# Layer A of a hybrid decoder step: the score products of the even units moved directly behind the chain's visits, those of the odd units gathered in two visits instead of five

## The chip, the cores and the metric

The kernel runs on one core of one Trainium2 chip. The metric is the device time of one execution in microseconds (us), lower is better. All arithmetic is fp32; the large weight products are done as three products of split numbers (a high part and a low part of the weight, and of the activation).

## What is computed

One inference step of a two-layer decoder trunk, for a prompt group (16 meta rows and 256 prompt rows, L = 272) and a sample group (8 rows), N = 280 columns together, model width 2048, branch width 4096. Layer A is RWKV-7 time mixing, layer B is sliding-window attention. The change is in layer A, whose reference is a scan over the rows with one 64 by 64 state per head:

```python
def rwkv7_step(S, inp):
    r, d, k, v, kk, b = inp
    sa = jnp.einsum('bhij,bhj->bhi', S, kk)
    S = S * d[:, :, None, :] - sa[..., None] * b[:, :, None, :] + v[..., None] * k[:, :, None, :]
    return S, jnp.einsum('bhij,bhj->bhi', S, r)
```

Before the scan stand the projections r, k, v, z (`jnp.einsum('btpd,pde->btpe', xm[:, :, :4], w_rkvz)`, four matrices of 2048 by 4096) and two small low-rank products for the decay and for a; behind it a group norm per head, a gate with silu(z) and the output projection of 4096 by 2048.

## The kernel before, in words

**The scan in chunks.** The kernel does not step through 272 rows. It cuts them into five chunks (four of 64 rows, one of 16) and solves each chunk with matrix products. A unit is 4 heads (two tiles of 128 partitions, two heads in each); there are 16 units, and two units, an even and an odd one, make a pair. For each unit:

- `prep` (line 803) loads k, r, v and the key norms from DRAM, does the low-rank products (`ps_l`), the decays and the small tiles for the sample group (`sm`, `ps_sm`) and the bonus (`ps_bo`). `prep_e` (line 901) builds the factors `KB` and `E`.
- `scores` (line 927) forms the products of `KB` with `E`. Two blocks of 8 matmuls each (line 959, tile `ps_sc`) take two chunks each; a third block of 4 (line 976) takes the short chunk; then two groups of 10 transposes (line 996, `ps_bk`) turn `KB`. What leaves PSUM after a block: three copies on ScalarE for each half (lines 964 to 966, into `ND` and `N12`) and two masked products on VectorE (lines 967 and 969, back into `E` and into `RB`). The transposes leave by ScalarE copies into `BK` (line 998).

For each pair:

- `substitute` (line 1000) inverts 16 by 16 triangles on GpSimd and VectorE and lays the result into the diagonal of the tile `TT` with four ScalarE activations (line 1032).
- `solve` (line 1036) extends that to 64 by 64 in four visits of many small matmuls (`ps_so`, lines 1049, 1055, 1067, 1076), each with copies out between them.
- `chain` (line 1104) walks through the five chunks. A chunk has three visits: `ps_wu` and `ps_sy` from the state (lines 1133 and 1137), `ps_wu` with `TT` (line 1148) after a ScalarE copy `W`, and `ps_sy` (lines 1151 and 1153) after the copies `X`; then VectorE updates the state `FS`.
- `group_norm` (line 1195) finishes the rows of the pair and writes them to DRAM.

**The stream that carries the time.** All this is small work beside the large weight products, which `products` yields (line 650): for every weight tile a ScalarE cast makes the high part `whi` (line 177), VectorE makes the low part `wlo` (line 178), and TensorE does three matmuls of 128 by 128 against 280 columns (lines 199 to 201). `products` yields after every 6 of these matmuls; this is called a step here.

**Who decides the order.** `drive` (line 567) goes from step to step. At each step it asks every stream (epilogues, the main stream, preps, decodes, late gates and side streams) whether its turn has come, lets it record its instructions, and then lets `products` record the next 6 matmuls. A stream says with `yield n, need` that it wants its next turn n steps later and only when `need` holds. The order of TensorE is written out by this: it runs its instructions as they were recorded. The order on VectorE, ScalarE, GpSimd and the DMA queue of SyncE is chosen by a scheduler from what was recorded, with priorities (the main stream stands 2000 ahead). So a stream's instructions on TensorE come as a block between two steps; this block is called a visit here.

The main stream (`main`, line 610) runs a pair's `chain`, then the odd `scores` of the next pair, then its `solve`. The even `scores` of the next pair run as a side stream (`even_scores`, line 637), beside the chain, at steps of their own:

```python
        gap = iter((8, 3, 4, 3, 3) if odd else (8, 6, 6, 5, 4))
        turn = iter((0, odd, 0, odd, 0))
```

`gap` is the number of steps ahead of each of the five visits; `turn` picks the PSUM banks: the two banks of pool `pe`, or (in the second and fourth visit of an odd unit) one bank each of pools `pc` and `py`, which the chain uses otherwise.

Of the kernel before, what the change touches and what calls it, by code (L numbers as in the profile page):

```python
# [10 lines left out]
F32 = mybir.dt.float32  # L11
# [9 lines left out]
E = 4096  # L21
# [82 lines left out]
class Kernel:  # L104
# [462 lines left out]
    def drive(self, products, streams, begun, ahead=2000):  # L567
        self.samples = False
        live = [[g, *begun.get(g, (0, None))] for g in streams]

        now = streams[:2]
        more = True
        with self.pe_order():
            while more or self.later or len(live) > 1:
                for s in list(live):
# [15 lines left out]
                self.pos += 1  # L591

# [210 lines left out]
    def prep(self, u):  # L803
# [5 lines left out]
        p0 = 2 * u  # L809
# [3 lines left out]
        wa, ws = [], []  # L813
# [27 lines left out]
        self.spread(kk, self.kr[u // 4][4 * u % 16:4 * u % 16 + 4])  # L841
        for j in range(2):
# [29 lines left out]
        vT = w("vT", 4)  # L872
        dma(vT, self.vd[b][:, sl])
# [4 lines left out]
        yield 8, self.pp_free  # L878
# [48 lines left out]
    def scores(self, u):  # L927
# [3 lines left out]
        gap = iter((8, 3, 4, 3, 3) if odd else (8, 6, 6, 5, 4))  # L931
        turn = iter((0, odd, 0, odd, 0))
        banks = lambda nm: [self.bank(p, f"ps_{nm[0]}{q}{nm[1]}") for q, p in
                            enumerate((self.pc, self.py) if next(turn) else (self.pe, self.pe))]
# [14 lines left out]
        for c0 in (0, 2):  # L949
            cs = slice(c0, c0 + 2)  # L950
            yield next(gap)
            ps = [b.rearrange("p (a c t) -> p a c t", a=2, c=2) for b in banks(("sc", f"{c0}_{u}"))]

            with self.pe_order():
                for j in range(2):
                    for c in range(2):
                        for q in (1, 0):
                            o = 128 * (c0 + c)
                            nc.tensor.matmul(ps[q][:, j, c], KB[H(q), j, c0 + c, 64 * q:64 * q + 128],
                                             E[q][H(q), j, o:o + 128], start=True, stop=True)  # L960
# [10 lines left out]
        yield next(gap)  # L971
        ps = [b[:, :64].rearrange("p (a h t) -> p a h t", a=2, h=2) for b in banks(("sc", f"4_{u}"))]
        with self.pe_order():
# [4 lines left out]
        for q in range(2):  # L978
            pv, kr, br = ps[q], H(1 - q), H(q)
            r1 = slice(64 * q, 64 * q + 32)  # L980
            m = self.cst(C_MASK, 128, kr).rearrange("p (h t) -> p h t", h=2)[:, :, 0:16]
            A.copy(self.ND[r1, 16 + i0 // 4:18 + i0 // 4, 0:16], pv[r1, :, 0])
            tt(E[q][kr, :, 512:544].rearrange("p a (h t) -> p a h t", h=2), pv[kr],
               m.unsqueeze(1).to_broadcast((64, 2, 2, 16)), op=MU)
            tt(RB[br, :, 256:272], pv[br, :, 1],
               self.cst(C_MASK + 64, 16, br).unsqueeze(1).to_broadcast((64, 2, 16)), op=MU)
        if odd:
            self.substitute(u // 2)

        for j in range(2):  # L990
            yield next(gap)
            ps = [b[:, :320].rearrange("p (c t) -> p c t", c=5) for b in banks(("bk", f"{j}_{u}"))]
            with self.pe_order():
                for c in range(5):
                    for q in (1, 0):
# [857 lines left out]
```

## Time and profile before

| | us |
|---|---|
| median of 3 runs | 2206.55 |
| lowest and highest run | 2203.35 and 2210.55 |
| the profiled execution's own time | 2211.88 |
| its span from first to last instruction | 2209.9 |
| TensorE busy (share of the span) | 2122.6 (96%) |
| VectorE busy | 1711.5 (77%) |
| ScalarE busy | 1283.1 (58%) |
| GpSimd busy | 76.1 (3%) |

The granted TensorE clock is 0.988 of full speed over the span. The span has three parts: a first stage up to about 170 us, layer A's mixed stage (weight products with prep, scores, solve and chain between) up to about 1360 us, and then the output projection of layer A and all of layer B. The fp32 matmuls of the small work appear as two records each in the profile, so 8 matmuls are 16 records; transposes and the large products appear as one. In a row of the timeline, the first number is the start, the second the time from the start to the end of the merged records, and the shape behind the operation's name is first the part of the array that the weights fill (rows * columns) and then the moving operand. Ends on TensorE are modelled, starts are not: the time that a visit takes is read from the starts of the rows around it.

### The profile page before, as it was taken

The numbers are of one execution on the slowest core, as the hardware profiler recorded it, in microseconds if no ns is written. First come the engines' busy times: TensorE is split into PE (matmuls) and PEld (weight loads), VectorE is DVE, ScalarE is ACT, GpSimd is POOL, SyncE is SP. The second block draws the span as 40 slices with busy tenths as digits, with TensorE's granted clock in tenths as the row PEclk, the third lists the DMA queues.
The fourth block names the chain that finished last, engine by engine and source line by source line (L and its number), as shares of the span: only waits on it lengthen the run. The fifth ranks groups of instructions, "written<-read, shape, count | busy, mean of one in ns | idle before, by whom it ended". The sixth has DMA issues, their size and how long they took to land. (4 is left out here: it accounts for less than half of the span.)

```text
span 2209.9 us, 56367 instructions
## 1 busy us (share of the span) xinstructions
PE 2122.6 (96%) x21596; PEld 2013.0 (91%) x21596; DVE 1711.5 (77%) x4138; ACT 1283.1 (58%) x2961; POOL 76.1 (3%) x102
## 2 busy tenths in 40 slices
PE   6999999899999999989999999999999999999997
PEld 4898889899999898989998999999999999999997
DVE  5875756687778786789878787887888888888885
ACT  3556765577576665667766444564565556555443
POOL 0010000000000000000100000110000000000000
PEclk9999999999999999999999999999999999999999
DMA  7988576658675668766655858777554554577774
GB/s 238 342 262 252 174 224 208 197 173 259 198 227 177 186 211 260 228 211 185 200 176 155 275 181 272 239 215 208 154 162 144 154 157 129 164 213 241 230 226 136
DMA packets 424886, 455.40 MB, mean 206 GB/s; under 512 B 64280, under 2 KB 383320, under 8 KB 424224
## 3 DMA queue, kind: packets, MB, share of 16 engines
q1 hardware_dynamic: 423800, 449.51, 65.6%
q8 instruction: 169, 2.77, 0.5%
q10 hardware_dynamic: 816, 2.29, 0.3%
q14 instruction: 101, 0.83, 0.1%
HBM read 385.08 MB, written 70.73 MB: 206 GB/s over the span
## 5 line engine op out<-in xcount | busy, mean ns | idle before, releaser
L199 PE MATMUL ps_z<-mhlm,whi_z 128*128 128x280 f32 x512 | 159.5, 311 | 0.0
L199 PE MATMUL ps_q<-bmh,whi_qb 128*128 128x264 f32 x512 | 150.6, 294 | 1.8 <-ACT whi_qb L177 1.8
L201 PE MATMUL ps_z<-mhlm,wlo_z 128*128 128x280 f32 x512 | 150.6, 294 | 0.8 <-DVE wlo_z L178 0.8
L200 PE MATMUL ps_z<-mhlm,whi_z 128*128 128x280 f32 x512 | 150.5, 294 | 0.0
L201 PE MATMUL ps_q<-bmh,wlo_qb 128*128 128x264 f32 x512 | 146.5, 286 | 1.1 <-DVE wlo_qb L178 1.1
L199 PE MATMUL ps_z<-bmh,whi_zb 128*128 128x264 f32 x512 | 147.5, 288 | 0.0
L200 PE MATMUL ps_q<-bml,whi_qb 128*128 128x264 f32 x512 | 146.1, 285 | 0.0
L200 PE MATMUL ps_z<-bml,whi_zb 128*128 128x264 f32 x512 | 145.4, 284 | 0.0
L201 PE MATMUL ps_z<-bmh,wlo_zb 128*128 128x264 f32 x512 | 145.4, 284 | 0.0
L199 PE MATMUL ps_ob<-ghi,whi_ob 128*128 128x264 f32 x512 | 145.2, 284 | 0.0
L201 PE MATMUL ps_ob<-ghi,wlo_ob 128*128 128x264 f32 x512 | 144.8, 285 | 0.0
L200 PE MATMUL ps_ob<-glo,whi_ob 128*128 128x264 f32 x512 | 144.5, 283 | 0.0
L177 ACT CAST whi_ob<-raw_ob 128x512 fp32r<-128x512 f32 x128 | 79.2, 621 | 97.0 <-PE ps_ob L200 78.7
L178 DVE TENSOR_TENSOR wlo_r<-raw_r,whi_r 128x512 fp32r<-128x512 f32 x128 | 87.1, 687 | 60.8 <-ACT whi_r L177 59.2
L177 ACT CAST whi_oa<-raw_oa 128x512 fp32r<-128x512 f32 x128 | 78.3, 621 | 89.5 <-DMA raw_oa<-a_w_out 35.4
L178 DVE TENSOR_TENSOR wlo_v<-raw_v,whi_v 128x512 fp32r<-128x512 f32 x128 | 87.0, 687 | 52.7 <-ACT whi_v L177 51.1
L199 PE MATMUL ps_v<-mhlm,whi_v 128*128 128x280 f32 x384 | 122.5, 319 | 0.7 <-ACT whi_v L177 0.7
L199 PE MATMUL ps_k<-mhlm,whi_k 128*128 128x280 f32 x384 | 120.6, 314 | 0.0
L178 DVE TENSOR_TENSOR wlo_k<-raw_k,whi_k 128x512 fp32r<-128x512 f32 x112 | 76.2, 688 | 53.8 <-ACT whi_k L177 51.8
L178 DVE TENSOR_TENSOR wlo_z<-raw_z,whi_z 128x512 fp32r<-128x512 f32 x128 | 86.8, 685 | 36.5 <-ACT whi_z L177 36.3
L177 ACT CAST whi_zb<-raw_zb 128x512 fp32r<-128x512 f32 x128 | 78.3, 619 | 62.5 <-PE ps_z L200 41.9
L201 PE MATMUL ps_v<-mhlm,wlo_v 128*128 128x280 f32 x384 | 113.2, 295 | 0.2 <-DVE wlo_v L178 0.2
(479 smaller groups left out, 7725.2 us busy)
## 6 DMA issues: line engine op xcount, KB each, us to landing
raw_k<-a_w_rkvz SPq DMA_DIRECT2D x128, 256.0 KB
raw_v<-a_w_rkvz SPq DMA_DIRECT2D x128, 256.0 KB
raw_r<-a_w_rkvz SPq DMA_DIRECT2D x128, 256.0 KB
raw_z<-a_w_rkvz SPq DMA_DIRECT2D x128, 256.0 KB
raw_oa<-a_w_out SPq DMA_DIRECT2D x128, 256.0 KB
raw_qb<-b_w_qz SPq DMA_DIRECT2D x128, 256.0 KB
raw_zb<-b_w_qz SPq DMA_DIRECT2D x128, 256.0 KB
raw_ob<-b_w_o SPq DMA_DIRECT2D x128, 256.0 KB
```

Source lines behind the costliest of these rows:

```text
L177: self.nc.scalar.copy(hi, src)
L178: return self.nc.vector.tensor_tensor(lo, src, hi.bitcast(F32), op=ALU.subtract)
L199: mm(ps, wh, xh, start=start, stop=False)
L200: mm(ps, wh, xl, start=False, stop=False)
L201: return mm(ps, wl, xh, start=False, stop=stop)
```

## The change

Only the functions `drive`, `prep`, `scores`, `substitute`, `solve` and `chain` are touched. No instruction is added on any of the compute engines and none is removed; instructions are put in other places.

- **Even units.** The five visits become four, and each waits for `ride`: it is taken only at a step at which the chain has just recorded a visit (`vis == pos`), or when no chain is running. `drive` now asks the streams in a sorted order so that a riding stream comes last in its step. The gaps are 8, 6, 6, 5. The third visit holds the short block and the first group of transposes, which share the two banks (transposes in columns 0 to 319, the block in columns 320 to 383). All visits use the banks of `pe`.
- **Odd units.** Two visits: 8 steps after the chain both large blocks (the first into `pe`, the second into `pc` and `py`), 6 steps later the short block and both groups of transposes (`block`, `last` and `turned` record the matmuls, `block_out`, `last_out` and `turned_out` the same copies as before). `substitute` is recorded there, and `solve` begins 30 steps later (33 for the last two pairs) instead of 24 (27).
- **TT.** Its four diagonal activations move from `substitute` into `solve`, behind the first visit of `solve` and its copy `ET`.
- **Copies later.** In `prep` both low-rank weight loads are issued 3 steps ahead of their casts, the first work with the loaded `kk` comes 3 steps after its load, and the load of `vT` stands 3 steps ahead of the copies that read it, ahead of the decays for the units 0 to 3. The step counts behind are cut by the same amounts (7 to 4, 8 to 5).

```diff
@@ drive
+        self.vis, self.chain_on = -1, False
-                for s in list(live):
+                for s in sorted(live, key=lambda s: 0 if s[0] in now else 1 if s[2] == self.ride else 2):
...
+    def ride(self):
+        return self.vis == self.pos or not self.chain_on
@@ prep
             dma(raw, I[wn][0, :, p0 * 128:p0 * 128 + 256])
+            raws.append(raw)
+        if u:
+            yield 3
+        for i, raw in enumerate(raws):
...
-                yield 3 if i or j else 7 if u else 14, self.pp_free
+                yield 3 if i or j else 4 if u else 14, self.pp_free
...
         self.spread(kk, self.kr[u // 4][4 * u % 16:4 * u % 16 + 4])
+        if u < 4:
+            vT = w("vT", 4)
+            dma(vT, self.vd[b][:, sl])
+        yield 3
...
         if u >= 4:
             yield 0, self.after(0, ('g', u // 2 - 2))
-        vT = w("vT", 4)
-        dma(vT, self.vd[b][:, sl])
+            vT = w("vT", 4)
+            dma(vT, self.vd[b][:, sl])
+            yield 3
...
-        yield 8, self.pp_free
+        yield 5, self.pp_free
@@ scores
+        wide = lambda nm: [self.bank(p, f"ps_{nm}{q}_{u}") for q, p in enumerate((self.pc, self.py))]
+        near = lambda nm: [self.bank(self.pe, f"ps_{nm}{q}_{u}") for q in range(2)]
...
+        if odd:
+            yield 8
+            with self.pe_order():
+                p0 = block(0, near("sca"))
+                p2 = block(2, wide("scb"))
+            block_out(*p0)
+            block_out(*p2)
+            yield 6
+            with self.pe_order():
+                banks = near("sc4")
+                p4 = last([b[:, 320:384] for b in banks])
+                t0 = turned(0, banks)
+                t1 = turned(1, wide("bkb"))
+            last_out(p4)
+            self.substitute(u // 2)
+            turned_out(*t0)
+            turned_out(*t1)
+            return
+        for c0 in (0, 2):
+            yield 8 - c0, self.ride
+            with self.pe_order():
+                p = block(c0, near(f"sc{c0}"))
+            block_out(*p)
+        yield 6, self.ride
+        with self.pe_order():
+            banks = near("sc4")
+            p4 = last([b[:, 320:384] for b in banks])
+            t = turned(0, banks)
+        last_out(p4)
+        turned_out(*t)
+        yield 5, self.ride
+        with self.pe_order():
+            t = turned(1, near("bkb"))
+        turned_out(*t)
@@ substitute
-        TT = rp.tile([128, 20, 64], F32, tag="TT", name=f"TT{o}")
-        for b in range(4):
-            A.activation(TT[:, :, 16 * b:16 * b + 16], TR[:, :, 0:20].rearrange("p t i -> p i t"), AF.Copy,
-                         scale=self.cst(C_M64 + 16 * b, 1))
@@ solve
-        yield 24 if o < 5 else 27
+        yield 30 if o < 5 else 33
...
         V.tensor_copy(ET, ps[:, 0:256].rearrange("p (i s) -> p i s", s=16))
+        TT = self.TT = rp.tile([128, 20, 64], F32, tag="TT", name=f"TT{o}")
+        for b in range(4):
+            A.activation(TT[:, :, 16 * b:16 * b + 16], TR[:, :, 0:20].rearrange("p t i -> p i t"), AF.Copy,
+                         scale=self.cst(C_M64 + 16 * b, 1))
         yield 4
@@ chain, at its three visits
+            self.vis, self.chain_on = self.pos, True
+            self.vis = self.pos
+            self.vis, self.chain_on = self.pos, c < 4
```

More of the change, by code (lines that the diff above doesn't have):

```diff
@@ L930, in scores @@
         odd = u % 2
[L931 to L934, printed above, removed]
         V, A, G = nc.vector, nc.scalar, nc.gpsimd
@@ L970, in scores, with last @@
                    bc(self.cst(C_MASK + 64, 64, br), 64, 2, 2, 64), op=MU)
-        yield next(gap)
-        ps = [b[:, :64].rearrange("p (a h t) -> p a h t", a=2, h=2) for b in banks(("sc", f"4_{u}"))]
-        with self.pe_order():
+        def last(outs):
+            ps = [b.rearrange("p (a h t) -> p a h t", a=2, h=2) for b in outs]
             for j in range(2):
@@ L977, in scores @@
                                      start=True, stop=True)
[L978 to L995, printed above, removed]
-                        nc.tensor.transpose(ps[q][:, c], KB[H(q), j, c, 64 * q:64 * q + 128], self.ident[H(q), H(q)])
+            return ps
+        def last_out(ps):
+            for q in range(2):
+                pv, kr, br = ps[q], H(1 - q), H(q)
+                r1 = slice(64 * q, 64 * q + 32)
+                m = self.cst(C_MASK, 128, kr).rearrange("p (h t) -> p h t", h=2)[:, :, 0:16]
+                A.copy(self.ND[r1, 16 + i0 // 4:18 + i0 // 4, 0:16], pv[r1, :, 0])
+                tt(E[q][kr, :, 512:544].rearrange("p a (h t) -> p a h t", h=2), pv[kr],
+                   m.unsqueeze(1).to_broadcast((64, 2, 2, 16)), op=MU)
+                tt(RB[br, :, 256:272], pv[br, :, 1],
+                   self.cst(C_MASK + 64, 16, br).unsqueeze(1).to_broadcast((64, 2, 16)), op=MU)
@@ L1029, in substitute @@
         V.transpose(TR.rearrange("p t i -> p (t i)"), NL)
[L1030 to L1034 removed]
+        self.TN, self.TR = TN, TR
     def solve(self, o):
```

32 lines of the change are left out of this document (19 added, 13 removed).

## The prediction

> **What bounds the kernel now.** I read the page's busy times first, then the busy times of the middle stage alone, then TensorE's waits, and last the timeline of single visits on TensorE, because the page says nothing on what a visit costs.
>
> ```profile
> PE 2122.6 (96%) x21596; PEld 2013.0 (91%) x21596; DVE 1711.5 (77%) x4138; ACT 1283.1 (58%) x2961; POOL 76.1 (3%) x102
> ```
>
> ```profile
> 170.00:1360.00 1190.00, 1143.02 (x13855) 1072.61 (x13854) 900.24 (x2022) 757.20 (x1799) 37.64 (x47) 0.98 0.68 210
> ```
>
> TensorE is the bound, and in layer A's mixed stage (the second row: its length, then busy TensorE, weight loads, VectorE, ScalarE, GpSimd) it is idle for only 1190.0 - 1143.0 = 47 us. The change touches nothing outside this stage. So it can gain in two ways: fewer or cheaper visits, or less of these 47 us. They are scattered over many short waits, of which these are the ones that the change comes near:
>
> ```profile
> PE ps_so L1049 <- DVE TN L1028: 4.8, 3, 3.3
> PE ps_vt L797 <- ACT vk L799: 3.9, 2, 2.5
> PE ps_o L199 <- ACT whi_oa L177: 2.8, 1, 2.8
> PE ps_so L1055 <- DVE ET L1051: 2.5, 2, 2.1
> PE ps_bk L996 <- DVE RB L985: 1.6, 2, 1.2
> ```
>
> What a visit costs beside its matmuls is in the timeline of TensorE. The first rows are a chain's third visit that by chance has a score block behind it; then come a chain's first visit, a score block alone, a chain's second visit with transposes behind it by chance, and transposes alone:
>
> ```profile
> 317.95 0.29 PE L201 MATMUL ps_k<-mhlm,wlo_k 128*128 128x280 f32 x1
> 318.18 0.69 PE L1151 MATMUL ps_sy<-X,BK 128*64 128x64 f32 x16
> 318.79 0.68 PE L1153 MATMUL ps_sy<-X,RB 64*64 64x64 f32 x16
> 319.40 1.16 PE L959 MATMUL ps_sc<-E,KB 64*128 64x128 f32 x16
> 320.49 0.40 PE L199 MATMUL ps_k<-mhlm,whi_k 128*128 128x280 f32 x1
> ...
> 324.55 0.69 PE L1133 MATMUL ps_wu<-X,E 128*64 128x64 f32 x16
> 325.07 0.64 PE L1137 MATMUL ps_sy<-X,E 128*64 128x64 f32 x16
> ...
> 326.00 0.29 PE L201 MATMUL ps_k<-mhlm,wlo_k 128*128 128x280 f32 x1
> ...
> 326.38 0.29 PE L201 MATMUL ps_k<-mhlm,wlo_k 128*128 128x280 f32 x1
> 326.60 1.16 PE L959 MATMUL ps_sc<-E,KB 64*128 64x128 f32 x16
> 327.69 0.40 PE L199 MATMUL ps_k<-mhlm,whi_k 128*128 128x280 f32 x1
> 327.93 0.29 PE L200 MATMUL ps_k<-mhlm,whi_k 128*128 128x280 f32 x1
> ...
> 341.60 0.68 PE L1148 MATMUL ps_wu<-W,TT 64*64 64x64 f32 x16
> 342.21 0.53 PE L996 MATMUL ps_bk<-consts,KB 64*128 64x64 f32 x10
> ```
>
> Between visits three large matmuls take 326.38 - 326.00 = 0.38, so 0.13 each, and a step of six is 0.77. Around the lone block: the last large matmul starts 0.22 ahead of it instead of 0.13 (entry: 0.09), the block runs 327.69 - 326.60 = 1.09, and the second large matmul behind it starts 0.24 after the first instead of 0.13 (exit: 0.11). Behind the chain's visit the same block again takes 320.49 - 319.40 = 1.09, with no entry and no exit of its own. So a joined visit saves 0.09 + 0.11 = **0.20 us**, though the tile of the array changes (64\*64 to 64\*128). Where the tile does not change, it saves more: 16 records followed by others of the same tile take 325.07 - 324.55 = 0.52, followed by another tile 342.21 - 341.60 = 0.61, and 318.79 - 318.18 is 0.61 too. A change of tile thus costs 0.09, and a join without one saves 0.20 + 0.09 = **0.29 us**.
>
> The Trainium skill, TensorEngine Tiling (Array Packing), section Tiling Modes, says that a change of the tiling mode drains TensorE, while a change of the tile within a mode does not. By it the joins between unlike tiles would be worth little; the rows agree that a change costs something, with 0.09, but it is less than an exit and an entry.
>
> **The change part by part.**
>
> *Joined visits.* I counted joins in the instruction order of the two built programs; both have the same matmuls. Before, 6 score or transpose groups stand by chance directly behind a chain's group. After, 28 do, all with a change of tile: 18 score groups behind `ps_sy` and 3 behind `ps_wu`, 7 transpose groups behind `ps_sy`. That is 22 more at 0.20: 4.4 us. Groups of one tile (64\*128) that now touch: the two large blocks of the 8 odd units, the short block with the first transposes in all 16 units, the first with the second transposes in the 8 odd units: 32 at 0.29: 9.3 us. Sum: **13.7 us less on TensorE**, all of it on the path, since TensorE is the path. Bounds: for unlike joins behind `ps_wu` and `ps_sy` of 128\*64 no row exists; from nothing to 0.20 each. For like joins no score or transpose row exists either; between 0.20, the unlike price, and 0.36. The upper end: if the 16 records of a block started as densely as those of `ps_wu` inside a visit, the 1.09 of the block would fall by no more than 0.16 (its 1.16 less the last record's own time, over 15 gaps, times 16, is near 0.93). So 6 to 16 us; I take 13.7, nearest to the rows.
>
> *Odd units, bursts.* Both blocks leave PSUM together, and the second visit needs `pe` empty for the short block and `pc` and `py` for the second transposes.
>
> ```profile
> L967 DVE TENSOR_TENSOR E<-ps_sc,consts 64x512 f32<-64x512 f32 x64 | 43.8, 684 | 18.9 <-ACT N L966 14.1 <-PE ps_r L200 2.6 <-PE ps_z L201 1.2
> L969 DVE TENSOR_TENSOR RB<-ps_sc,consts 64x256 f32<-64x256 f32 x64 | 27.0, 422 | 0.9
> L178 DVE TENSOR_TENSOR wlo_v<-raw_v,whi_v 128x512 fp32r<-128x512 f32 x128 | 87.0, 687 | 52.7 <-ACT whi_v L177 51.1 <-PE ps_v L201 1.1
> ```
>
> VectorE needs 4 x 0.684 + 4 x 0.422 = 4.4 us for both blocks, and one or two low parts of 0.69 fall between: 5.1 to 5.8. The time from the end of the first visit to the first write into `pc` is 6 steps, 4.6, and about 0.9 for the short block and the first transposes: 5.5. That just fits when VectorE is free. It is not always:
>
> ```profile
> 382.38 1.16 PE L959 MATMUL ps_sc<-E,KB 64*128 64x128 f32 x16
> ```
>
> ```profile
> 383.59 1.76 DVE L1205 TENSOR_TENSOR Y<-Y,gvar 128x1536 f32<-128x1536 f32 x1
> 388.99 0.42 DVE L969 TENSOR_TENSOR RB<-ps_sc,consts 64x256 f32<-64x256 f32 x1
> ```
>
> Here the group norm's 1.76 us stood ahead, and the first block was out only 389.41 - 382.38 = 7.0 after it began. With the second block's 2.2 and one low part, 0.7, it is 9.9; the visit would want it at 2.2 + 5.5 = 7.7. Wait: 2.2. I estimate that two or three of eight units are like this: 5 us lost; bounds 0 and 8 x 2.2 = 17.6. Given back: the 1.6 of `ps_bk` on `RB` of the short block, since the next use of those banks is now `solve`, 30 steps later.
>
> *Even units, rides.* 28 visits of the chain get a block behind them. Queued behind it on ScalarE stand the chain's copies `X`:
>
> ```profile
> L965 ACT COPY ND<-ps_sc 32x128 f32<-32x128 f32 x64 | 16.5, 258 | 0.8
> L1150 ACT COPY X<-ps_wu 64x256 f32<-64x256 f32 x64 | 23.3, 365 | 18.2 <-PE ps_wu L1148 17.1
> L177 ACT CAST whi_v<-raw_v 128x512 fp32r<-128x512 f32 x128 | 78.5, 618 | 55.0 <-DMA raw_v<-a_w_rkvz 27.1 <-PE ps_v L200 19.5 <-PE ps_v L201 3.1
> ```
>
> In the built order six copies, 6 x 0.258 = 1.55, and a cast, 0.62, stand between `W` and the two `X`. They take 2.2 from the block's end; the chain's second visit begins two steps, 1.5, after it and needs some 0.8, so they are done when `X` may start. `X` takes 0.73, the third visit comes three steps, 2.3, later: 1.6 us of slack. Cost: nothing. Without that cover it is one for one, times 28.
>
> *TT.* Four activations move past the first visit of `solve`:
>
> ```profile
> L1032 ACT ACTIVATE TT<-TR,consts 128x320 f32<-128x320 f32 x32 | 25.4, 870 | 5.8 <-DVE TR L1029 5.8
> ```
>
> That is 3.5 us of ScalarE between the first and second visit, four steps or 3.1, and the first user is the copies behind the second. Those have seven steps, 5.4, to the third. So nothing is late. What goes is the 5.8 us in which ScalarE stood waiting for `TR` with casts and other copies queued behind. I credit 1.8 us of TensorE's waits behind it, an estimate; bounds 0 and the 7.3 of both `ps_so` rows above.
>
> *Loads.* SyncE's queue issues the same loads in nearly the same order; `vT` now stands three steps ahead of the copies from it. ScalarE's idle time for it, 15.9 us in 6 waits, is one source of late casts.
>
> ```profile
>   DMA vT<-vd: 15.9, 6
> ```
>
> But in the built order the copy from `vT` stands as many casts behind its load as before (counting weight loads on SyncE and casts on ScalarE), as the scheduler moved both. Cost and gain: nothing; bounds a gain of 3.9 (`ps_vt` above) and a loss of as much. The 3 steps ahead of the low-rank casts are taken out behind them. The chains end 8 steps earlier against the weight products, so the late gates and their loads meet other casts: 0, at most 2.8 either way (the `ps_o` row).
>
> **Sum.** -13.7 + 5.0 - 1.6 - 1.8 = -12.1. The profiled execution took 2211.88 (span 2209.9), 5.3 above the median of the three runs; I subtract from both: 2199.8 for a like execution, and **2194.5 us** against the median of 2206.55.
>
> **Rivals.**
>
> *Unlike joins save nothing.* If the drain at a change of tile from 128\*64 to 64\*128 costs a whole entry and exit, the 4.4 go: 2199. Against it speaks the block at 319.40. This is what the skill's rule, read strictly, gives. Chance 0.10.
>
> *All odd units wait.* If VectorE is late in all eight, 17.6 instead of 5.0: 2207, no change. For it: the fit of 5.1 to 5.8 into 5.5 is tight. Against: most low parts stand ahead of the burst in the built order, as casts run some four weight tiles ahead. Chance 0.14.
>
> *Slower: the rides hold the chain up.* The place is ScalarE between a block's copies and `X`, the price is one for one in 28 visits, and it decides once ScalarE is more than 1.6 late there. At 2.6 late each, 28 us are lost: 2222. Against: ScalarE is 757 of 1190 us busy. Chance 0.11.
>
> *More than forecast.* If the steps between loads and copies also take away the waits for `vT` and more of those for `TN` and `ET`, some 7 more: 2187. Chance 0.13.
>
> **How the numbers follow.** Forecast with 2189 to 2200 as its own range: 0.52. A change under 0.3% (6.6 us) is about what a measurement of this kernel cannot tell from none, so faster means below 2199.9. Faster: 0.52, 0.13, most of the unlike joins and a little of the third case: 0.73. Same: the rest of both: 0.16. Slower: 0.11. The range from 2184 to 2207 leaves out the rides and the outermost part of the better case.
>
> **What would show it.** The timeline of TensorE should show joined groups with starts 0.61 apart where the tile changes; a large block followed by another some 0.95 later, not 1.09; the short block and the transposes with no large matmul between. The second visit of odd units should show at most three waits for `E` or `RB`. `ps_bk`'s wait on `RB` of the short block, and ScalarE's wait for `TR` ahead of `TT`, should be gone. Idle time of TensorE in the mixed stage should stay between 43 and 53 us. The prediction is wrong if that idle time grows by over 8, with waits of `ps_sy` for `X` or of the transposes for `RB`, or if like joins save no more than 0.20.

## The result, and the profile after

The changed kernel takes 2243.65 us (median of four runs, 2238.49 to 2247.48) against 2208.55 for the kernel before on the same chip: a ratio of 1.0162, with a 95% interval of 1.0144 to 1.0180. It is slower by 35 us; 2194.5 had been predicted, with a range up to 2207. Its profiled execution took 2238.49 (span 2236.5, mean granted clock 0.978), that of the kernel before 2211.88 (span 2209.9, clock 0.988).

The page's line of busy times of the changed kernel tells nothing of it:

```profile
PE 2122.4 (95%) x21596; PEld 2022.3 (90%) x21596; DVE 1708.8 (76%) x4138; ACT 1285.1 (57%) x2961; POOL 72.2 (3%) x102
```

TensorE's busy time is what it was (2122.6). The loss shows in the mixed stage alone, in the table of busy times by stretch (changed kernel; length, then TensorE, weight loads, VectorE, ScalarE, GpSimd, granted clock, DMA share):

```profile
170.00:1360.00 1190.00, 1120.07 (x13712) 1058.99 (x13712) 884.89 (x1998) 750.28 (x1784) 33.34 (x47) 0.97 0.67 204
```

Two numbers of this row are worse than before: TensorE stands idle for 1190.0 - 1120.1 = 69.9 us instead of 47.0, and the granted clock is 0.97 instead of 0.98. TensorE's waits in this stage (changed kernel; who waits, for what, us in total, times, longest):

```profile
PE ps_so L1095 <- DVE TN L1078: 15.0, 3, 7.0
PE ps_so L1105 <- issue: 8.0, 4, 3.0
PE ps_wu L1184 <- ACT X L1220: 5.8, 5, 3.0
...
PE ps_so L1095 <- issue: 3.3, 1, 3.3
```

The first two visits of `solve` wait 15.0 + 8.0 + 3.3 = 26.3 us. In the kernel before, the same two waited 4.8 for `TN`, 2.5 for `ET` and, with no releaser named, 2.2 + 0.9, in all 10.4:

```profile
PE ps_so L1055 <- issue: 2.2, 3, 0.9
...
PE ps_so L1049 <- issue: 0.9, 1, 0.9
```

The waits with no releaser ("issue") are of another kind than those for `TN`: they are holes inside a visit. In the second visit at 427.20 of the changed kernel, 124 of the 128 records run, and then TensorE stands, though `ET` had been there since 425.99:

```profile
430.34 0.23 PE L1105 MATMUL ps_so<-TR,ET 32*16 32x16 f32 x4 [1.93 <-issue]
```

The other such waits of the two visits also fall between records of one visit; what they wait for, the profile does not show. No score or transpose visit of the changed kernel waits for `E` or `RB`.

The joins are there, as forecast. TensorE's timeline of the changed kernel: an odd unit's two large blocks, then, at another place, an even unit's block riding behind a chain's first visit:

```profile
931.48 0.29 PE L201 MATMUL ps_z<-mhlm,wlo_z 128*128 128x280 f32 x1
931.69 1.16 PE L968 MATMUL ps_sca<-E,KB 64*128 64x128 f32 x16
932.69 1.06 PE L968 MATMUL ps_scb<-E,KB 64*128 64x128 f32 x16
933.68 0.39 PE L199 MATMUL ps_z<-mhlm,whi_z 128*128 128x280 f32 x1
933.91 0.29 PE L200 MATMUL ps_z<-mhlm,whi_z 128*128 128x280 f32 x1
...
460.69 0.64 PE L1188 MATMUL ps_sy<-X,E 128*64 128x64 f32 x16
461.26 1.16 PE L968 MATMUL ps_sc<-E,KB 64*128 64x128 f32 x16
462.35 0.40 PE L199 MATMUL ps_v<-mhlm,whi_v 128*128 128x280 f32 x1
```

The two blocks start 1.00 apart, against 1.09 for a lone block, and share one entry and one exit: from the last large product to the second one behind them 933.91 - 931.48 = 2.43, less the two ordinary steps of 0.13 is 2.17. Two lone blocks cost 2 x 1.29 = 2.58, so this join saves 0.41. The riding block saves its entry and exit and still runs 1.09. So TensorE has less to do, and the time is lost in waiting and in the clock.

How much in each, I worked out from a table of busy times in stretches of one microsecond, 170 to 1410 us, 1240 rows for each kernel: idle time is what is not busy, and the time lost to the clock is the busy time times one minus the granted clock.

| profiled execution, us | before | after | difference |
|---|---|---|---|
| span | 2209.9 | 2236.5 | +26.6 |
| TensorE idle, 170 to 1410 | 47.2 | 76.1 | +28.9 |
| lost to the clock, 170 to 1410 | 18.7 | 33.2 | +14.5 |
| the rest of the span | 2144.0 | 2127.2 | -16.8 |

The rest is what the same work costs without waits: it fell by 16.8, where 13.7 had been worked out for the joins. The waits grew by 28.9, and the clock took another 14.5. Of the 28.9, the waits for `TN` are 15.0 - 4.8 = 10.2, the holes inside the solve visits 11.3 - 3.1 = 8.2, and the rest is spread over many short waits.

**What a late solve looks like.** The longest wait of the changed kernel, 7.00 us, from its timelines: one row of the DMA queue, two of ScalarE, three of VectorE and one of TensorE.

```profile
1109.89 0.41 SPq L886 DMA_DIRECT2D vT<-vd  x1
...
1115.07 0.20 ACT L891 COPY sm<-vT 128x16 f32<-128x16 f32 x1 [5.81 <-DMA vT<-vd]
1115.18 1.28 ACT L177 CAST whi_z<-raw_z 128x512 fp32r<-128x512 f32 x2
...
1115.82 0.69 DVE L178 TENSOR_TENSOR wlo_z<-raw_z,whi_z 128x512 fp32r<-128x512 f32 x1 [1.97 <-ACT whi_z L177]
1116.43 0.24 DVE L1074 TENSOR_TENSOR NL<-NL,stmp 128x88 f32<-128x88 f32 x1
...
1118.89 1.03 DVE L1078 STREAM_TRANSPOSE TN<-NL 128x512 f32<-128x512 f32 x1
...
1120.07 1.11 PE L1095 MATMUL ps_so<-TN,Noff 32*32 32x16 f32 x69 [7.00 <-DVE TN L1078]
```

Read upwards: TensorE waits for `TN`; the substitution that makes `TN` stands on VectorE behind a low part; the low part waits for a cast on ScalarE; and the cast stands in ScalarE's order behind a copy from `vT`, whose load was issued at 1109.89 and is there at 1115. ScalarE stands for 5.81 us. In these rows nothing overtakes the instruction that waits, on either engine, so a load that only prep needs holds up the solve. The kernel before has the same stall in the same pair, only shorter (one row each of ScalarE, VectorE and TensorE):

```profile
1114.26 0.21 ACT L877 COPY sm<-vT 128x16 f32<-128x16 f32 x1 [3.28 <-DMA vT<-vd]
...
1115.42 1.12 DVE L1028 STREAM_TRANSPOSE TN<-NL 128x512 f32<-128x512 f32 x1
...
1116.69 1.26 PE L1049 MATMUL ps_so<-TN,Noff 32*32 32x16 f32 x128 [0.41 <-DVE TN L1028]
```

There `TN` was done at 1116.54, and TensorE had come only 0.41 us too early. From such rows one can read, pair by pair, how long `TN` had been ready when the first solve visit began. In the kernel before it is 0.1, 0.9, 5.5, 3.1, 5.5, 0.1, 0.2 and 8.4 us. In the first, sixth and seventh pair there was nothing to give, and these are the three pairs in which the changed kernel waits for `TN`: 3.6, 4.3 and 7.0 us.

**The clock.** The same wait in stretches of 1 us (changed kernel, columns as above; the clock is the third number from the end):

```profile
1113.00:1114.00 1.00, 0.07 (x1) 0.00 (x0) 0.78 (x3) 0.00 (x0) 0.00 (x0) 1.00 0.92 264
1117.00:1118.00 1.00, 0.00 (x0) 0.00 (x0) 0.93 (x7) 0.21 (x1) 0.00 (x0) 0.98 0.03 10
1118.00:1119.00 1.00, 0.00 (x0) 0.00 (x0) 0.93 (x5) 0.00 (x0) 0.00 (x0) 0.50 0.53 90
1123.00:1124.00 1.00, 1.00 (x6) 1.00 (x6) 0.00 (x0) 1.00 (x2) 0.00 (x0) 0.50 0.00 0
1124.00:1125.00 1.00, 1.00 (x7) 1.00 (x7) 0.82 (x2) 0.27 (x2) 0.00 (x0) 0.61 0.06 16
1125.00:1126.00 1.00, 1.00 (x11) 1.00 (x10) 1.00 (x3) 0.97 (x3) 0.00 (x0) 1.00 0.05 10
```

TensorE runs dry at 1113.07. From 1118 on the granted clock is 0.50, and it stays there for some 4.7 us after the work is back at 1120.07: 2.4 us more are lost (half of the 3.9 up to 1124, and 0.39 of the next). Such drops to 0.50 come 9 times between 170 and 1410 us of the kernel before and 14 times after the change. The Trainium skill, TensorE: Matmul & The Clock Gate, section "What's actually happening", has two states, half clock after an idle window of about 3.4 us and full clock after one of sustained work; this stall agrees (half after 4.9 us idle, full again after 4.7 us of work). Seven of the nine drops of the kernel before come behind shorter waits; the last section shows two of them.

### The profile page after: what moved, and what is told of

Read it like the earlier page. It is cut to its first block, busy times and chain, and to the rows that moved or that the text cites. A ratio compares the mean times of both kernels' runs of the same rounds, so it can differ in the third digit from the quotient of the medians.

```text
span 2236.5 us, 56336 instructions
## 1 busy us (share of the span) xinstructions
PE 2122.4 (95%) x21596; PEld 2022.3 (90%) x21596; DVE 1708.8 (76%) x4138; ACT 1285.1 (57%) x2961; POOL 72.2 (3%) x102
## 4 chain that ended last, share of the span: by engine, by line
PE 51%; DMA 5%; DVE 4%; ACT 2%; issue 2%; SPq 0%; DVEq 0%; POOLq 0%; ACTq 0%
PE ps_z L199 5%; PE ps_z L200 4%; PE ps_z L201 4%; PE ps_ob L201 3%; PE ps_ob L200 3%; PE ps_ob L199 3%; PE ps_q L201 3%; PE ps_q L199 3%; PE ps_q L200 3%; DMA raw_oa<-a_w_out 1%; PE ps_oa L200 1%; PE ps_oa L201 1%; PE ps_oa L199 1%; PE ps_s L1699 1%; PE ps_o L199 1%
## 5 line engine op out<-in xcount | busy, mean ns | idle before, releaser
L201 PE MATMUL ps_k<-mhlm,wlo_k 128*128 128x280 f32 x384 | 113.5, 296 | 1.1 <-issue 1.1
L178 DVE TENSOR_TENSOR wlo_z<-raw_z,whi_z 128x512 fp32r<-128x512 f32 x128 | 86.8, 686 | 35.1 <-ACT whi_z L177 32.5
```

Source lines behind the costliest of these rows:

```text
L178: return self.nc.vector.tensor_tensor(lo, src, hi.bitcast(F32), op=ALU.subtract)
L201: return mm(ps, wl, xh, start=False, stop=stop)
```

## The experiments

My first theory was that the solve's `TN` had become late through one of four things: the moved TT diagonal, the later copies in `prep`, the rides, or the odd units' two visits. Ratios are to the kernel before on the same chip, with 95% intervals.

**The parts one by one.** `joins_only` is the changed kernel with `prep` and TT of before:

```diff
 substitute
+        TT = rp.tile([128, 20, 64], F32, tag="TT", name=f"TT{o}")
+        for b in range(4):
+            A.activation(TT[:, :, 16 * b:16 * b + 16], TR[:, :, 0:20].rearrange("p t i -> p i t"), AF.Copy,
...
 solve
-        TT = self.TT = rp.tile([128, 20, 64], F32, tag="TT", name=f"TT{o}")
-        for b in range(4):
-            A.activation(TT[:, :, 16 * b:16 * b + 16], TR[:, :, 0:20].rearrange("p t i -> p i t"), AF.Copy,
...
 prep
-        if u:
-            yield 3
...
```

> Only the even units' rides and the odd units' two visits; TT's diagonal and the whole of prep as before. If the moved TT diagonal and the later copies bring the loss, this gains what the joins save: some 14 us less than before, 2192 to 2198. If the joins themselves bring it (less real time from substitute to solve, rides that hold the chain up), it stays near the changed kernel: 2236 to 2246. In between, the loss has several sources.

Measured: 2245.38, 1.0167 (1.0144 to 1.0189). `after_tt_before` undoes the first half of that diff alone, `after_prep_before` the second half alone:

> The changed kernel with TT's diagonal back in substitute. If the four activations between the first two solve visits bring the loss, the waits of the second solve visit (8.0 us) and part of those of the first (15.0 us) go and the time falls by 15 us or more, to 2210 to 2230. If they don't matter: 2238 to 2248. If the move was a help, as the prediction credited it with 1.8 us, it gets a little slower.

> The changed kernel with prep as before (loads, kk, vT and step counts). If the later copies in prep shift the order of VectorE and ScalarE and so make TN, X and the low-rank factors late, most of the loss goes: about 2200 to 2215. If they have nothing to do with it: 2238 to 2248.

Measured: 2245.06, 1.0158 (1.0131 to 1.0185), and 2245.63, 1.0167 (1.0146 to 1.0188). With TT back in `substitute` the waits of the first two solve visits are where they were:

```profile
PE ps_so L1099 <- DVE TN L1078: 14.9, 3, 6.4
PE ps_so L1105 <- issue: 8.5, 4, 3.0
```

`before_prep_after` puts the changed `prep` alone into the kernel before:

> The kernel before with the changed prep alone. If the later copies in prep bring the loss by themselves: 2225 to 2250. If they matter only together with the tighter scores and solve, or not at all: 2200 to 2212.

Measured: 2210.0, 1.0011 (0.9997 to 1.0024). So TT's move and the later copies neither cost nor gain anything that can be measured; the joins bring the loss.

**Odd or even units, rides or not.** `odd_only` gives the kernel before the odd branch of the changed `scores` and the solve 30 steps behind it, with the even units in their five visits; `even_only` gives it the even units' four riding visits; `no_ride` has both but leaves the rides out:

```diff
 no_ride, even units, against joins_only
-            yield 8 - c0, self.ride
+            yield 8 - c0
...
-        yield 6, self.ride
+        yield 6
...
-        yield 5, self.ride
+        yield 5
```

> The kernel before with the odd units' two visits (solve 30 steps behind) and nothing else; even units in five visits at their own steps, prep and TT as before. If the odd units' bursts and the shorter real time to the solve bring the loss: 2230 to 2246. If the rides bring it: some 5 us less than before by its own joins (24 like joins at 0.29 less one or two waits), 2200 to 2205.

> The kernel before with the even units' four riding visits and nothing else; odd units in five visits, solve 24 steps behind, prep and TT as before. If the rides bring the loss: 2230 to 2246, with waits for X, for whi and at the solve. If the odd units bring it: some 6 us less than before, 2199 to 2204.

> The joins without the rides: the odd units' two visits, and the even units' four visits at their own steps (8, 6, 6, 5) whether or not the chain has a visit; prep and TT as before. If riding itself brings the loss (blocks of an even unit bunched in three neighbouring visits of a chunk, copies ahead of X): 2200 to 2210. If the odd units or the four visits bring it: 2236 to 2246.

Measured: `odd_only` 2243.67, 1.0166 (1.0147 to 1.0186); `even_only` 2207.02, 1.0001 (0.9989 to 1.0012); `no_ride` 2236.18, 1.0128 (1.0105 to 1.0152). The odd units' two visits alone bring a loss as large as the whole. `odd_only`'s mixed stage and its first waits:

```profile
170.00:1360.00 1190.00, 1117.73 (x13668) 1049.77 (x13667) 882.76 (x1989) 746.89 (x1782) 34.32 (x47) 0.97 0.66 203
```

```profile
PE ps_so L1087 <- DVE TN L1066: 13.0, 4, 5.8
PE ps_wu L1172 <- ACT X L1208: 8.5, 5, 4.0
PE ps_so L1093 <- issue: 7.9, 5, 3.9
PE ps_so L1114 <- ACT ET L1109: 4.2, 2, 3.3
```

The rides are harmless by themselves, though what their joins save (6.7 us by the prices above, 4.6 in the table below) does not appear in its time. With the odd units' joins beside them they cost 9 us (2245.38 of `joins_only` against 2236.18).

**Is it late TN?** Two ways to give `TN` more time, with TensorE's joins untouched. `solve_later` moves the solve, `after_half_substitute` shortens what makes `TN` (it leaves out half of the rounds of the substitution, and so a part of the computation):

```diff
 solve_later
-        yield 30 if o < 5 else 33
+        yield 36 if o < 5 else 39
 after_half_substitute
-        for s in range(1, 15):
+        for s in range(1, 8):
```

> The changed kernel with solve beginning 36 steps (39 for the last two pairs) behind the odd units' last visit instead of 30 (33). If too little time from substitute to the first solve visit brings the loss, the first solve visit's 15.0 us of waits go: 2222 to 2230 or less. If the loss sits in the rides: 2238 to 2250.

> The changed kernel with the substitution's loop cut from 14 rounds to 7 (the triangles of 16 by 16 are not fully inverted, so this leaves out part of the computation): some 4 us less of VectorE's chain of small operations in each pair, TensorE's order untouched. If VectorE's fullness ahead of TN is the cause, the waits of the first solve visit go and the time falls by 15 to 30 us: 2214 to 2229. If the bursts and the PSUM banks are the cause: 2236 to 2246.

Measured: 2216.82, 1.0038 (1.0021 to 1.0054), and 2216.38, 1.0043 (1.0028 to 1.0058). Each takes away 27 of the 35 us. With the halved substitution no visit waits for `TN` any more, while the second solve visit still waits:

```profile
PE ps_so L1105 <- issue: 8.4, 5, 2.6
```

So late `TN` is shown to be worth 27 us in the changed kernel, and it is not the number of steps as such, since the second kernel keeps them. It isn't simply lighter work on VectorE either: the halved substitution takes 20 us off VectorE's busy time (1688.6 against 1708.8), the later solve nothing (1710.9). A part of the 27 the kernel before pays too, in its 4.8 us of such waits; so late `TN` is shown to be one cause of the 35 us, and not the only one. With the later solve the wait for `TN` is 3.0 us, and the stage's end comes up instead, in the waits of `solve_later`:

```profile
PE ps_oa L199 <- ACT ghi L177: 10.3, 2, 6.4
...
PE ps_so L1095 <- DVE TN L1078: 3.0, 1, 3.0
```

The output projection waits for the last gated rows; every pair is 6 steps later.

**Does the kernel before stand at an edge?** Its solve three steps earlier, and six later:

```diff
-        yield 24 if o < 5 else 27
+        yield 21 if o < 5 else 24        (before_solve_21)
+        yield 30 if o < 5 else 33        (before_solve_30)
```

> The kernel before, nothing joined, with solve 21 steps behind the odd scores instead of 24 (24 instead of 27 for the last two pairs): some 2.3 us less of TensorE's time between the short block and the first solve visit. Theory: VectorE is full between the chain's end and TN, the kernel before stands at the edge, and any shortening there turns into waits for TN and a lower clock behind them. Then: 2218 to 2235, with 10 us or more of ps_so waiting for TN. Rival, the joined bursts themselves do the harm (PSUM banks, copies that leave together): no change, 2203 to 2211.

> The kernel before with solve 30 steps behind the odd scores instead of 24 (33 instead of 27). If the kernel before already loses by TN (4.8 us of waits and the clock behind them), it gains 3 to 10 us: 2197 to 2205. If later solves push other work back as much: 2206 to 2216.

Measured: 2218.97, 1.0058 (1.0041 to 1.0074), and 2226.3, 1.0085 (1.0058 to 1.0111). It loses in both directions: 24 is the best of the three. Later is bad at least for the reason just seen (waits of `before_solve_30`):

```profile
PE ps_oa L199 <- ACT ghi L177: 12.0, 3, 7.3
```

Earlier is bad, but the cause that I had written down is not borne out: its profiled execution shows 4.2 us of waits for `TN`, no more than before, and that execution, 2210.86, was the fastest of its four. Where the others lose isn't known.

**Can the joins be kept and the loss avoided?** `no_ride_solve_36` is `no_ride` with the solve 36 and 39 steps behind. Three kernels fit the solve's steps to each pair, and one brings only the last pair of `solve_later` back:

```diff
-        yield 30 if o < 5 else 33
+        yield (34, 34, 29, 31, 28, 39, 38, 24)[o]             (no_ride_tuned, on no_ride)
+        yield (34, 32, 29, 32, 30, 39, 39, 24)[o]             (after_tuned)
+        yield 36 if o < 5 else 39 if o < 7 else 24            (solve_later_last_early)
-        yield 24 if o < 5 else 27
+        yield (26, 26, 22, 23, 22, 30, 29, 19)[o]             (before_tuned)
```

> The joins without the rides and with solve 36 steps behind (39 for the last two pairs), prep and TT as before. With the solve waits gone and the rides left out, what the joins save is left: 2198 to 2208. If rides and solve cure the same waits: 2214 to 2222, as with the later solve alone.

> Joins without rides; solve begins 34, 34, 29, 31, 28, 39, 38 and 24 steps behind the odd units' last visit in the eight pairs: later where TN was late, earlier where TN had been done for 5 to 10 us, and the last pair early so that the output projection does not wait for it. If late TN on one side and a late end on the other are all that eats the joins, what they save is left: 2190 to 2202. If the joins only move waits about: 2205 to 2215.

> The changed kernel, rides and all, with solve 34, 32, 29, 32, 30, 39, 39 and 24 steps behind. Same question with the rides: 2190 to 2202 if they cost nothing, some 9 us more than without them if the difference between the runs with and without rides (2245 against 2236) is their price: 2199 to 2211.

> The kernel with the later solve (36 and 39 steps), its last pair alone brought back to 24. That kernel's output projection stood 10.3 us waiting for the last gated rows; if that wait and the lower clock behind it are its remaining loss, this falls by 8 to 16 us: 2201 to 2209. If 15 steps fewer for one pair do not bring the rows early enough, or make TN of that pair late: 2212 to 2220.

> Control: the kernel before, nothing joined, with solve 26, 26, 22, 23, 22, 30, 29 and 19 steps behind instead of 24 and 27. If fitting the steps to TN is what gains and not the joins, this gains as much as the joined kernels do: 2192 to 2202. If the kernel before was fitted already: 2204 to 2216.

Measured: `no_ride_solve_36` 2209.5, 1.0008 (0.9995 to 1.0020); `no_ride_tuned` 2219.54, 1.0059 (1.0038 to 1.0080); `after_tuned` 2214.08, 1.0024 (1.0012 to 1.0036); `solve_later_last_early` 2214.34, 1.0030 (1.0018 to 1.0042); `before_tuned` 2211.48, 1.0012 (0.9999 to 1.0026). None reaches 2202. The fitted steps were read from the waits of kernels with other steps, and the waits came up elsewhere. In all three, the early solve of the last pair (24 or 19 steps) found its `TN` late by 3.1 to 4.1 us. In `no_ride_tuned` the low-rank products wait for `cl`, and `TN` is late twice:

```profile
PE ps_l L199 <- ACT cl L833: 7.2, 5, 3.2
...
PE ps_so L1090 <- DVE TN L1069: 4.8, 2, 4.1
```

In `solve_later_last_early` the wait for the gated rows is halved, as meant:

```profile
PE ps_so L1095 <- DVE TN L1078: 6.3, 2, 4.2
PE ps_oa L199 <- ACT ghi L177: 4.8, 1, 4.8
```

Its time hardly fell all the same, and the first row says why: the longest of its waits for `TN`, 4.2 us, is that of the pair brought forward, as the expectation had named for this case. One wait was exchanged for another. `no_ride_solve_36` has no wait for `TN` at all, but 12.6 us of waits for the gated rows. One kernel is free of both, `after_half_substitute`, and it takes 2216.38: late `TN` and a late end are not all that eats the joins.

**Which join of the odd units?** Each made alone on the kernel before (shown against `odd_only`, which has both):

```diff
 odd_blocks_joined, against odd_only
-            yield 6
+            yield 7
             with self.pe_order():
-                banks = near("sc4")
-                p4 = last([b[:, 320:384] for b in banks])
-                t0 = turned(0, banks)
-                t1 = turned(1, wide("bkb"))
+                p4 = last([b[:, :64] for b in near("sc4")])
             last_out(p4)
             self.substitute(u // 2)
+            yield 5
+            with self.pe_order():
+                t0 = turned(0, near("bka"))
+                t1 = turned(1, wide("bkb"))
...
-        yield 30 if o < 5 else 33
+        yield 25 if o < 5 else 28
 odd_short_joined, against odd_only
-                p0 = block(0, near("sca"))
-                p2 = block(2, wide("scb"))
-            block_out(*p0)
-            block_out(*p2)
-            yield 6
+                p = block(0, near("sca"))
+            block_out(*p)
+            yield 3
+            with self.pe_order():
+                p = block(2, wide("scb"))
+            block_out(*p)
+            yield 4
```

> Even units, prep and TT as before; of the odd units only the two large blocks are joined and, 5 steps behind the substitution, the two groups of transposes with each other; the short block stays alone, 7 steps behind the blocks as before, and solve is 30 steps behind it as before. TensorE's transposes so still lie between the substitution and the solve. If it is the work taken out from there, and the copies of the transposes falling together with the substitution, that hurts: 2198 to 2208, the joins' 4.6 us saved. If it is the two large blocks leaving PSUM together: 2225 to 2245.

> The other half: the two large blocks apart as before (8 and 3 steps), and 4 steps later the short block with both groups of transposes in one visit, solve 30 steps behind it. If the transposes gone from between substitution and solve bring the loss: 2225 to 2245. If the two large blocks do: 2198 to 2208.

Measured: 2207.46, 0.9994 (0.9979 to 1.0009), and 2205.43, 0.9990 (0.9974 to 1.0007). Neither hurts; both together cost 36 us. Their mixed stages and waits for `TN`, the first kernel, then the second:

```profile
170.00:1360.00 1190.00, 1143.84 (x13883) 1077.26 (x13882) 905.71 (x2028) 760.24 (x1801) 34.34 (x47) 0.98 0.69 210
```

```profile
PE ps_so L1088 <- DVE TN L1067: 3.9, 2, 2.7
```

```profile
170.00:1360.00 1190.00, 1142.18 (x13922) 1074.60 (x13921) 902.53 (x2032) 761.02 (x1804) 36.42 (x47) 0.99 0.69 211
```

```profile
PE ps_so L1089 <- DVE TN L1068: 5.0, 4, 2.0
```

Both expectations that named a single guilty join fell. What the two together have and neither alone: from the chain's end to the solve there are 8 + 6 + 30 = 44 steps instead of 45, and the time of three joins is gone from there as well. From the prices above that is 0.77 + 3 x 0.29 = 1.6 us a pair or more, against 2 x 0.29 = 0.6 for each single kernel. `odd_only` waits for `TN` in the first, second, sixth and seventh pair (2.2, 0.9, 5.8 and 4.2 us), the four that had less than 1 us to give in the kernel before. But these waits are only 13.0 - 4.8 = 8.2 us of the 30.4 by which its idle time grew (table below); the others, for `X`, for `ET` and in the holes of the second solve visit, have no tested cause. A threshold between 0.6 and 1.6 us would explain the rest. It isn't shown: three steps taken from the kernel before are 2.3 us a pair and cost only 11.

**All kernels side by side.** The same account as in the table above, one profiled execution each; the medians contain other executions of the same kernel, which differ by up to 17 us.

| kernel | median | idle | lost to the clock | rest of the span |
|---|---|---|---|---|
| before | 2208.55 | 47.2 | 18.7 | 2144.0 |
| before_solve_21 | 2218.97 | 47.1 | 18.5 | 2143.3 |
| before_solve_30 | 2226.3 | 60.2 | 25.7 | 2140.4 |
| before_prep_after | 2210.0 | 48.1 | 16.9 | 2140.1 |
| before_tuned | 2211.48 | 51.5 | 16.6 | 2139.5 |
| odd_short_joined | 2205.43 | 47.9 | 13.3 | 2138.4 |
| odd_blocks_joined | 2207.46 | 46.2 | 23.0 | 2135.3 |
| even_only | 2207.02 | 46.7 | 15.7 | 2136.9 |
| odd_only | 2243.67 | 77.6 | 28.1 | 2134.3 |
| no_ride | 2236.18 | 72.7 | 27.4 | 2133.9 |
| no_ride_solve_36 | 2209.5 | 55.8 | 17.7 | 2133.1 |
| no_ride_tuned | 2219.54 | 64.2 | 23.7 | 2132.8 |
| after_half_substitute | 2216.38 | 61.2 | 24.9 | 2130.1 |
| after_tuned | 2214.08 | 56.0 | 28.6 | 2129.2 |
| solve_later_last_early | 2214.34 | 61.9 | 24.4 | 2127.9 |
| after_tt_before | 2245.06 | 74.7 | 30.8 | 2127.6 |
| after_prep_before | 2245.63 | 76.2 | 35.1 | 2127.4 |
| after | 2243.65 | 76.1 | 33.2 | 2127.2 |
| solve_later | 2216.82 | 63.0 | 19.5 | 2127.0 |
| joins_only | 2245.38 | 81.7 | 37.1 | 2126.6 |

The last column sorts the kernels by their joins alone: 2139.5 to 2144.0 without any (mean 2141.5), 2126.6 to 2130.1 with all of them (mean 2127.9). So the joins save 13.6 us on average. The three kernels with all joins but the rides lie between (mean 2133.3): the rides save 5.4 of the 13.6, the joins of one tile 8.2. The two columns before it decide the time, and in no kernel with all the joins did they stay as low as before. No version measured faster than the kernel before.

## Why the prediction was wrong, point by point

- **Joined visits, -13.7: right in kind and size.** The rest of the span fell by 13.6 over the groups of kernels: 8.2 for the joins of one tile (9.3 in the sum) and 5.4 for the unlike ones (4.4). That the total comes out to 0.1 us is luck, as the kernels of one group differ by up to 4.5. The two large blocks shown save 0.41 instead of 0.29, the ride behind `ps_sy` leaves the block's 1.09 as forecast. The rival by which unlike joins save nothing has those 5.4 us against it, and a row: `ps_sc` starts 0.57 after `ps_sy` at 461.26, less than the 0.61 forecast for a change of tile. The Trainium skill (TensorEngine Tiling (Array Packing), Tiling Modes) has a change of mode drain TensorE; if it does, the drain is no dearer than that.
- **That this is "all of it on the path, since TensorE is the path": the step that failed.** It reads 96% busy as "every microsecond saved on TensorE is one saved in the span". But TensorE runs beside VectorE, ScalarE and loads, and what makes `TN` there did not become shorter. Shorter visits let TensorE come sooner to `solve`, and it stood there: 15.0 us for `TN` instead of 4.8. The prediction had quoted that row of 4.8 as a thing to gain from; it showed that in some pairs the solve had no slack at all. It never worked out `TN`'s slack per pair, which was 0.1, 0.1 and 0.2 us in the three pairs that then waited. Idle time grew by 28.9 us in all and the clock took 14.5, so the 16.8 saved in work became a loss; with `TN` made sooner or the solve later, 27 us come back. For the other 18.7 us of idle time the cause stays open.
- **"the next use of those banks is now `solve`, 30 steps later": only the steps were counted.** In the kernel before, two visits of transposes also stood in those 30 steps.
- **Odd units, bursts, +5.0: wrong in place.** In the changed kernel no visit waited for `E` or `RB`; the feared collision in PSUM did not come there. (Two second groups of transposes wait 2.6 us for the copies `BK`, a row that `odd_only` does not have.) The loss of the odd units lay behind it: at the solve, as far as it was traced. The 1.6 given back for `RB` of the short block came, for no row of that wait is left.
- **Rides at nothing: undecided.** Alone they neither gain nor lose, so what their joins save is paid back somewhere; with the other joins they cost 9 us in one pair of kernels (`no_ride` and `joins_only`) and 7 in another (`no_ride_solve_36`, 2209.5, and `solve_later`, 2216.82, which has the moved TT and the later copies as well), and in the fitted pair (`no_ride_tuned` and `after_tuned`, with other steps) they don't.
- **TT, credit -1.8: not borne out.** Undoing the move changes nothing that can be told (2245.06 against 2243.65; 1.8 us lie inside the interval). The wait that the move was to remove did not go: ahead of `TT`, ScalarE waits 14.9 us for `TR` instead of 5.8.
- **Loads and copies at nothing: right** (1.0011 with the changed `prep` alone). The shift of the late gates was not tried apart.
- **A wait was priced at its own length.** The waits grew by 28.9 us and the clock behind them took 14.5 more: half as much again in these two executions, and 9.4 on 30.4 in `odd_only`. No term and no rival held that.
- **The rivals.** Slower had a chance of 0.11, and its mechanism (ScalarE's copies ahead of `X` of the third visit) has no row of waits in the changed kernel. The 5.8 us of waits for `X` there are of a chunk's first visit, for the copy of the state (line 1220); `joins_only` has 6.0 and `no_ride` 0.7 of them, but `odd_only`, without rides, 8.5. The mechanism that was shown, a shortened TensorE that meets `TN` too early, was not among the rivals. The sign "wrong if idle time grows by over 8" was the right one, though the waits it named were not.

What stays open: why both joins of the odd units together cost 36 us and neither alone anything; and what lies behind the holes inside the solve visits, for which the profile names no releaser.

## What to carry to other kernels

Before crediting time saved on the busiest engine, take from the trace, for each of its visits, how long its operands had been ready when it came; where that slack is near zero, the saving can turn into a wait. Count that slack in microseconds and not in steps of a written order, since shorter visits make the steps shorter too. Price a TensorE wait at more than its length where the granted clock drops behind it, and split a measured change into work, idle time and clock first: here that showed a forecast gain that was really there and a loss more than twice as large beside it.

## What the runs showed of the hardware that I had not expected

The clock drops without a long wait as well. The kernel before, TensorE's timeline and then stretches of 1 us at a first solve visit:

```profile
837.60 0.32 PE L1049 MATMUL ps_so<-TN,Noff 32*32 32x16 f32 x15 [0.91 <-issue]
...
838.13 0.44 PE L200 MATMUL ps_k<-mhlm,whi_k 128*128 128x280 f32 x1
838.36 0.44 PE L201 MATMUL ps_k<-mhlm,wlo_k 128*128 128x280 f32 x1
```

```profile
836.00:837.00 1.00, 0.68 (x81) 0.59 (x70) 0.00 (x0) 0.00 (x0) 0.00 (x0) 1.00 1.09 355
837.00:838.00 1.00, 0.41 (x16) 0.37 (x16) 0.00 (x0) 0.15 (x2) 0.00 (x0) 1.00 1.03 403
838.00:839.00 1.00, 1.00 (x5) 1.00 (x6) 0.40 (x1) 0.57 (x2) 0.00 (x0) 0.50 1.06 399
```

A wait of 0.91 us inside a visit of 64 matmuls of 32 by 32 (128 records) was enough: the clock is 0.50 from 838 on, and the large products follow each other at 0.23 instead of 0.13. By the Trainium skill's rule (TensorE: Matmul & The Clock Gate, "What's actually happening") an idle window of about 3.4 us would be needed; the longest idle time here is 0.91.

It is not a matter of the small matmuls alone. The same kernel, where large products and three transposes run up to 1344.36:

```profile
1347.21 0.60 PE L199 MATMUL ps_o<-mhlm,whi_oa 128*128 128x280 f32 x1 [2.85 <-ACT whi_oa L177]
```

The stretch from 1346 to 1347 has a clock of 0.79 and the next one 0.50, so the clock fell some 2.2 us after TensorE had run dry. Of the nine drops between 170 and 1410 us of this kernel, two stand at waits of over 3 us (3.97 and 3.34); at the other seven the longest wait is between 0.91 and 2.85. What decides between a short wait that costs the clock and one that doesn't was not tried.
